# Large tiles at multiples of 256 bytes, and new tables of how far weight splits run ahead, in a two-layer encoder trunk

## The chip, the cores and the metric

The kernel runs on one core of a Trainium2 chip. The metric is the device time of one execution in microseconds (us). Before the change the median of three runs is 920.38 us (919.2 to 921.86). The engines are called PE (TensorE matmul), PEld (its weight loads), DVE (VectorE), ACT (ScalarE), POOL (GpSimd) and SP (SyncE, which only issues transfers here).

## What is computed

The reference takes 256 tokens of width 1024 through two layers. Each layer is a feed-forward network (FFN), an attention mix, and a second FFN, each behind an RMS norm and added to the residual; a final norm follows.

```
x = x + 0.5 * swiglu(rms_norm(x, ffn1_norm[l]), ffn1_w_gate[l], ffn1_w_up[l], ffn1_w_down[l])
proj = rms_norm(x, mix_norm[l]) @ w_in[l]            # 1024 -> 2304
out_a = windowed_gqa_sink(qa, ka, va, sink[l], slopes_a)
out_b = differential_attention(qb, kb, vb, lam, slopes_b)
x = x + concatenate([out_a, norm(out_b)]) @ w_out[l]  # 1024 -> 1024
x = x + 0.5 * swiglu(rms_norm(x, ffn2_norm[l]), ffn2_w_gate[l], ffn2_w_up[l], ffn2_w_down[l])

def swiglu(h, w_gate, w_up, w_down):                  # 1024 -> 2816 -> 1024
    return (jax.nn.silu(h @ w_gate) * (h @ w_up)) @ w_down
```

Everything is float32. The weights are about 41 million numbers, of which the four FFNs hold 35 million.

## The kernel before, in words

**Splits.** A float32 weight tile (`raw`, 128 partitions x 2048 numbers, 8 KB a partition, six buffers) is loaded from HBM and cut in two halves. Each half becomes two tiles of 4 KB a partition of the type float32r (`w`, from the pool `s4` of 28 buffers): ACT casts the raw half into the high part (`act.copy`, in the profile CAST w<-raw), and DVE subtracts that from the raw half for the low part (TENSOR_TENSOR w<-raw,w). One product of a chunk of 128 rows is then three matmuls: high by high, low by high, high by low (`tokens`, `prod`). This pair of instructions is called a split below.

**Groups of seven products.** An FFN has 2816 hidden columns, in groups of 512 (`ffn_specs`, `ffn`). For the groups in `SEVEN` gate and up are computed for the two halves of tokens with seven block products instead of eight (`seven`, `by_seven`, `by_sevens`). With a and d the two halves of the rows of gate, and b and c those of up, the weights wanted are a, d, a+b, a+b+c, b+c, c and a+b+c+d. The sums are made in place in the raw tiles: b is added into a by a transfer that POOL issues (`gather`, an adding DMA, raw<-in_ffn_w_up_dram from POOL), which waits until both halves of a are split; c into b by another; c into a+b (`plus(c, a)`) and d into a+b+c (`plus(d, a)`) by an addition on DVE (raw<-raw,raw). PE's order in such a group is a, dn1, d, dn0, ab, abc, bc, c, abcd (for layer 0's first FFN from its second group on, for the other three FFNs from the first, where dn1 begins with the second group): dn0 and dn1 are down-projections of hidden columns of groups before, 24 matmuls each, the others 12 each.

**Evacuations.** Between products ACT and DVE empty PSUM banks: ACT copies bank A to bank Q and starts silu from it (COPY ps<-ps, ACTIVATE tmp<-ps,r), DVE forms u0 and u1 (tmp<-ps,tmp and tmp<-xy,tmp) and the hidden activations (s<-tmp,hr,tmp); PE transposes these, and ACT and DVE split the result (`turn_one`: CAST s<-xy, then s<-xy,s on DVE, of which PE needs the low part in dn0).

**What sets the order.** Program order on ACT and DVE is fixed by the order in which Python writes it. Splits are numbered by halves, and `ahead(n)` writes all splits, additions, adding DMAs and loads up to half n that are not yet written. Between two evacuations `go()` calls `ahead` with the next number of a row of the table `LEAD`: rows `next`, `more` and `last` serve the first, middle and last group of seven products, with the number of the FFN (0 to 3) behind; rows `open` and `close` serve the first and last steps of an FFN, through `lead` and `weights`. A larger number puts more splits before the evacuation that follows. PE's own order does not depend on the tables.

```
def go(table=None):
    if table is not None:
        upto[0] = 2 * at["use"] - (2 if table == "next" else 0)
        more[0] = iter(LEAD[table + str(which)])
    ahead(upto[0] + next(more[0]))
```

**Places.** Tiles stand in a partition in the order of their pools: `const`, `wp` (raw), `s4` (weights, hidden activations, normed inputs), `tp` (tmp, q and v, where the sums of inputs lie, and small ones). The constants end so that the first raw tile begins at byte 32160 of a partition, 160 bytes past a multiple of 256; the raw and `s4` tiles and the `tmp`, `q` and `v` tiles all stand 160 past one.

Of the kernel before, what the change touches and what calls it, by code (L numbers as in the profile page):

```python
# [9 lines left out]
F32 = mybir.dt.float32  # L10
# [4 lines left out]
P = 128  # L15
# [16 lines left out]
ORDER = (("a", "d", "dn0", "ab", "abc", "bc", "c", "abcd"),  # L32
         ("a", "dn1", "d", "dn0", "ab", "abc", "bc", "c", "abcd"))
LEAD = dict(start=(2, 7, 8, 6),
            open0=(2, 0, 0, 2, 3, 6, 8, 6, 5, 6, 1, 10, 1, 5, 7, 6, 8, 0),
            next1=(10, 10, 14, 14, 14, 17, 19, 19, 20, 24),
            next2=(10, 10, 14, 14, 14, 17, 19, 19, 20, 24),
            next3=(10, 10, 14, 14, 14, 17, 19, 19, 20, 24),
            more0=(1, 9, 9, 11, 15, 15, 19, 19, 19, 23, 25),
            more1=(7, 8, 8, 9, 9, 14, 18, 18, 19, 19, 20),  # L40
            more2=(7, 8, 8, 9, 9, 14, 18, 18, 19, 19, 20),
            more3=(7, 8, 8, 9, 9, 14, 18, 18, 19, 19, 20),
            last0=(7, 8, 8, 15, 15, 15, 15, 17, 19, 19, 19),
            last1=(3, 7, 7, 9, 14, 14, 14, 17, 20, 20, 23),
            last2=(3, 7, 7, 9, 14, 14, 14, 17, 20, 20, 23),
            last3=(3, 7, 7, 9, 14, 14, 14, 17, 20, 20, 23),
            open1=(1, 6, 7, 3, 4, 11, 5, 9),
            open2=(10, 7, 6, 8, 2, 0, 9, 8),
            open3=(9, 3, -1, 1, 5, 1, 9, 9),
            close0=(10, 5, 11, 1, -1, 8, 11, 2, 8, 12, 0, -1, 3),  # L50
            close1=(1, 8, 12, 3, 3, 7, 7, 12, 6, 9, 10, 6, 1),
            close2=(1, 8, 12, 3, 3, 7, 7, 12, 6, 9, 10, 6, 1),
            close3=(1, 8, 12, 3, 3, 7, 7, 12, 6, 9, 10, 6, 1),
            mix=(10, 0, 0, 0, 11, 3, 2, 6, 8, 9, 5, 1, 3, 0, 3, 5, 2, 2, 4, 5, 4, 8, 1, 10, 4, 9))


# [1 line left out]
def trunk(ctx: ExitStack, tc: tile.TileContext, x, n1, g1, u1, d1, nm, w_in, sink,  # L58
# [23 lines left out]
    const = ctx.enter_context(tc.tile_pool(name="const", bufs=1))  # L82
    wp = ctx.enter_context(tc.tile_pool(name="wp", bufs=1))
    s4 = ctx.enter_context(tc.tile_pool(name="s4", bufs=N_S4))
    tp = ctx.enter_context(tc.tile_pool(name="tp", bufs=1))
    ps = ctx.enter_context(tc.tile_pool(name="ps", bufs=1, space=bass.MemoryType.PSUM))

    uid = [0]

# [493 lines left out]
    lsum = const.tile([P, 2, DEPTH], F32, name="lsum")  # L583
    nlam = const.tile([P, DEPTH], F32, name="nlam")
    gsub = const.tile([P, DEPTH], F32, name="gsub")
    slopeA = [2.0 ** -(h + 1) for h in range(8)]
    slopeB = [2.0 ** -(2 * (h + 1)) for h in range(4)]
    lam_init = [0.8 - 0.6 * math.exp(-0.3 * l) for l in range(DEPTH)]
# [748 lines left out]
```

## Time and profile before

The profiled execution took 919.88 us, of which the span from the first to the last instruction is 918.1.

| what | value |
|---|---|
| median of three runs | 920.38 us |
| profiled execution, and its span | 919.88 us, 918.1 us |
| ACT casts of weights (CAST w<-raw) | 457, 404.4 us busy |
| DVE low parts of weights (w<-raw,w) | 458, 477.7 us busy, 55.0 us idle before them |
| DVE additions of raw tiles | 30, 68.6 us busy |
| adding DMAs from POOL | 30 of 1024 KB, median 12.0 us from issue to landing |
| moved by DMA | 200.83 MB, mean 219 GB/s |

Busy shares say how long an engine worked, not what the end waits for. Matmuls overlap in time, so their pace is read from how many fit into a stretch. A transfer's time to landing includes its wait behind others on the same 16 DMA engines.

The four FFNs lie, in the span, from the start to about 172 us, from about 300 to 440, 480 to 610 and 755 to 911 us; the mixes lie between the first two and between the last two.

### The profile page before, as it was taken

The page shows a single profiled execution, that of the slowest core. Times are in us where ns is not written, and L with a number is a line of the kernel's source. Part 1 is how long each engine was busy: PE and PEld are TensorE (multiplying, and loading weights), DVE is VectorE, ACT ScalarE, POOL GpSimd, SP SyncE. Part 2 cuts the span into 40 slices and gives each one's busy share as a digit, 9 for nine tenths or more (in the row PEclk, how much of TensorE's full clock was granted, in tenths as well). Part 3 has the DMA queues.
Part 4 walks back from the last instruction along what each step waited for, and adds up shares of the span by engine and source line. Part 5 has one row for each costly group of instructions (what it writes and reads, how often), then busy time and mean ns, then how long its engine had stood idle before and what let it go on. Part 6 is the DMA issues. An engine that isn't in the chain of part 4 may idle for free.

```text
span 918.1 us, 12062 instructions
## 1 busy us (share of the span) xinstructions
PE 905.3 (99%) x4468; PEld 749.2 (82%) x4468; DVE 779.4 (85%) x1058; ACT 610.6 (67%) x970; POOL 61.4 (7%) x79
## 2 busy tenths in 40 slices
PE   9999999999999999999999999999999999999997
PEld 7888888888878888888888877888888888887786
DVE  5878989979896899989768898997888978989884
ACT  6847667666676667668456676676667776667660
POOL 0411010000001011010010010000000010010001
PEclk9999999999999999999999999999999999999999
DMA  9997898953156698899855898899501865898841
GB/s 328 344 257 225 267 241 286 314 133 140 47 197 172 172 259 256 252 251 346 296 106 182 217 291 259 224 357 262 176 36 48 305 143 176 210 297 265 213 156 47
DMA packets 114331, 200.83 MB, mean 219 GB/s; under 512 B 3678, under 2 KB 31648, under 8 KB 114272
## 3 DMA queue, kind: packets, MB, share of 16 engines
q1 hardware_dynamic: 97616, 167.66, 53.9%
q0 software_dynamic: 16096, 31.75, 19.5%
q8 instruction: 35, 0.57, 0.3%
q10 hardware_dynamic: 560, 0.66, 0.2%
q14 instruction: 24, 0.20, 0.1%
HBM read 199.00 MB, written 1.05 MB: 218 GB/s over the span
## 4 chain that ended last, share of the span: by engine, by line
PE 67%; DVE 13%; DMA 11%; issue 4%; ACT 4%; SPq 0%; POOLq 0%; POOL 0%; DVEq 0%; ACTq 0%
PE ps L73 48%; PE xy L73 19%; DMA raw<-in_ffn_w_up_dram 10%; DVE w L73 8%; DVE raw L73 3%; ACT w L73 3%; DVE s L73 1%; DMA xk<-in_x_dram 1%; DVE tmp L73 1%; ACT s L73 0%; SPq L187 0%; ACT junk L73 0%; ACT tmp L73 0%; DVE xk L73 0%; POOLq L1332 0%
## 5 line engine op out<-in xcount | busy, mean ns | idle before, releaser
L73 DVE TENSOR_TENSOR w<-raw,w 128x1024 fp32r<-128x1024 f32 (+1 forms) x458 | 477.7, 1097 | 55.0 <-ACT w L73 49.3
L73 PE MATMUL ps<-w,s 128*128 128x512 f32 (+1 forms) x1974 | 461.1, 390 | 1.5 <-ACT ps L73 1.4
L73 ACT CAST w<-raw 128x1024 fp32r<-128x1024 f32 (+1 forms) x457 | 404.4, 952 | 75.7 <-DVE raw L73 50.8
L73 PEld LDWEIGHTS ps<-w,s 128*128 128x128 f32 x1974 | 364.4, 188 | 81.0 <-ACT ps L73 3.1
L73 PE MATMUL xy<-w,s 128*128 128x512 f32 x600 | 143.4, 392 | 0.0
L73 PEld LDWEIGHTS xy<-w,s 128*128 128x128 f32 x600 | 111.5, 188 | 23.1
L73 PE MATMUL ps<-w,q 128*128 128x512 f32 x396 | 96.1, 392 | 2.4 <-DVE w L73 1.3
L73 PEld LDWEIGHTS ps<-w,q 128*128 128x128 f32 x396 | 73.8, 188 | 20.5 <-DVE w L73 4.1
L73 PE MATMUL ps<-s,w 128*128 128x512 f32 (+1 forms) x384 | 69.8, 338 | 0.0
L73 DVE TENSOR_TENSOR raw<-raw,raw 128x2048 f32<-128x2048 f32 x30 | 68.6, 2287 | 0.5
L73 PEld LDWEIGHTS ps<-s,w 128*128 128x128 f32 x384 | 58.7, 188 | 8.4
L73 POOL DMA_DIRECT2D raw<-in_ffn_w_up_dram x30 | 38.9, 1346 | 365.6 <-DVE w L73 292.0
L73 ACT ACTIVATE s<-ps,gcol 128x256 fp32r<-128x256 f32 (+1 forms) x80 | 31.4, 479 | 42.6 <-PE ps L73 42.6
L73 PE MATMUL xy<-w,v 128*128 128x512 f32 x180 | 43.2, 389 | 0.0
L73 ACT ACTIVATE tmp<-ps,r 128x512 f32<-128x512 f32 x34 | 22.9, 687 | 29.0 <-PE ps L73 28.6
L73 PEld LDWEIGHTS xy<-w,v 128*128 128x128 f32 x180 | 33.8, 188 | 7.0
L73 DVE SCALAR_TENSOR_TENSOR s<-ps,gcol,s 128x256 fp32r<-128x256 f32 x48 | 20.4, 478 | 20.2 <-ACT s L73 20.2
L73 ACT ACTIVATE s<-s,negm 128x256 f32<-128x256 f32 x64 | 31.8, 498 | 5.3 <-DVE negm L73 5.3
L73 PE MATMUL xy<-w,q 128*128 128x512 f32 x144 | 34.6, 389 | 0.0
L73 PEld LDWEIGHTS xy<-w,q 128*128 128x128 f32 x144 | 27.0, 188 | 5.6
L73 ACT CAST q<-tmp 128x512 fp32r<-128x512 f32 x20 | 12.4, 621 | 19.7 <-DVE tmp L73 19.4
L73 POOL TENSOR_TENSOR r<-ms,mhalf 128x2 f32<-128x2 f32 x6 | 5.1, 849 | 298.9 <-DVE ms L73 298.9
(131 smaller groups left out, 584.4 us busy)
## 6 DMA issues: line engine op xcount, KB each, us to landing
raw<-in_ffn_w_down_dram SPq DMA_DIRECT2D x44, 1024.0 KB, 7.2
raw<-in_ffn_w_gate_dram SPq DMA_DIRECT2D x39, 1024.0 KB, 5.6
raw<-in_ffn_w_up_dram SPq DMA_DIRECT2D x39, 1024.0 KB, 6.9
raw<-in_ffn_w_up_dram POOLq DMA_DIRECT2D x30, 1024.0 KB, 12.0
raw<-in_w_in_dram SPq DMA_DIRECT2D x14, 1024.0 KB, 8.5
raw<-in_ffn_w_gate_dram SPq DMA_DIRECT2D x8, 512.0 KB, 7.1
raw<-in_ffn_w_up_dram SPq DMA_DIRECT2D x8, 512.0 KB, 8.1
raw<-in_w_in_dram SPq DMA_DIRECT2D x8, 512.0 KB, 8.5
```

The lines of the kernel that those rows point to most:

```text
L73: ins = issue(*a, **k)
```

## The change

Two tiles that nothing reads or writes are added: 152 numbers (608 bytes) at the end of the constants, so that the first raw tile begins at byte 32768, and 64 numbers (256 bytes) at the head of `tp`. All `raw`, `s4`, `tmp`, `q` and `v` tiles then begin at multiples of 256 bytes. And the rows of `LEAD` are replaced, except `start` and `mix`; where FFNs 1 to 3 shared the numbers of a row, each has its own now.

```diff
-            open0=(2, 0, 0, 2, 3, 6, 8, 6, 5, 6, 1, 10, 1, 5, 7, 6, 8, 0),
+            open0=(7, 4, -1, 0, 6, 0, -1, 0, 5, 4, 10, 5, 5, 4, -1, 9, -1, -1),
...
-            more2=(7, 8, 8, 9, 9, 14, 18, 18, 19, 19, 20),
+            more2=(6, 8, 8, 10, 11, 15, 18, 19, 20, 20, 20),
...
+    tp.tile([P, 64], F32, tag="edge", bufs=1, name="edge_t")
...
+    const.tile([P, 152], F32, name="edge")
```

Three places show what the rows do. All are in layer 1's first FFN (FFN 2), between its second and third group of seven products, some 528 to 556 us into the span. Numbers in names count tiles as they are made, and differ between the two kernels for the same tile.

First, DVE in the third group. `raw_4656` before and `raw_4659` after are the tile that holds a, then a+b, then a+b+c; `s_968`, `s_969` before and `s_970`, `s_971` after are the transposed hidden activations. Before:

```order
L73 TENSOR_TENSOR w_4955<-raw_4656,w_4954 128x1024
L73 TENSOR_TENSOR s_968_4962<-xy_4434,s_968_4962 128x512
L73 TENSOR_TENSOR s_969_4969<-xy_4435,s_969_4969 128x512
L73 TENSOR_TENSOR w_4973<-raw_4656,w_4972 128x1024
L73 TENSOR_TENSOR raw_4656<-raw_4656,raw_4819 128x2048
L73 TENSOR_TENSOR w_5016<-raw_4656,w_5015 128x1024
```

And DVE at the same place after the change:

```order
L73 TENSOR_TENSOR w_4955<-raw_4659,w_4954 128x1024
L73 TENSOR_TENSOR w_4959<-raw_4659,w_4958 128x1024
L73 TENSOR_TENSOR raw_4659<-raw_4659,raw_4821 128x2048
L73 TENSOR_TENSOR s_970_4969<-xy_4436,s_970_4969 128x512
L73 TENSOR_TENSOR s_971_4976<-xy_4437,s_971_4976 128x512
L73 TENSOR_TENSOR w_4980<-raw_4659,w_4979 128x1024
```

The second split of a+b and the addition of c now stand before the two low halves of the hidden activations, which stood before them. The same swap stands in the second group of this FFN and in the second and third group of layer 0's second FFN.

Second, ACT at the end of the second group and the start of the third. `ps_4433` before and `ps_4435` after are bank Q. Before:

```order
L73 CAST w_4813<-raw_4656 128x1024
L73 COPY tmp_4835<-xy_4434 128x512
L73 COPY ps_4433<-ps_4432 128x512
L73 CAST w_4852<-raw_4656 128x1024
L73 ACTIVATE tmp_4885<-ps_4433,r_4335 128x512
L73 CAST w_4887<-raw_4663 128x1024
```

And ACT at the same place after the change:

```order
L73 CAST w_4817<-raw_4659 128x1024
L73 COPY tmp_4837<-xy_4436 128x512
L73 CAST w_4839<-raw_4659 128x1024
L73 COPY ps_4435<-ps_4434 128x512
L73 CAST w_4859<-raw_4713 128x1024
L73 ACTIVATE tmp_4891<-ps_4435,r_4333 128x512
```

The cast of the second half of a now stands before the copy into bank Q, and the cast of the next raw tile before the silu that reads Q once PE has added to it.

Third, DVE at that same end of the second group. `raw_4345` before and `raw_4343` after hold a+b+c and then a+b+c+d; the first row's raw tile is c. Before:

```order
L73 TENSOR_TENSOR w_4782<-raw_4563,w_4781 128x1024
L73 TENSOR_TENSOR raw_4345<-raw_4345,raw_4488 128x2048
L73 TENSOR_TENSOR w_4802<-raw_4563,w_4801 128x1024
L73 TENSOR_TENSOR w_4806<-raw_4345,w_4805 128x1024
L73 TENSOR_TENSOR w_4810<-raw_4345,w_4809 128x1024
```

And DVE there after the change:

```order
L73 TENSOR_TENSOR w_4784<-raw_4574,w_4783 128x1024
L73 TENSOR_TENSOR w_4788<-raw_4574,w_4787 128x1024
L73 TENSOR_TENSOR raw_4343<-raw_4343,raw_4490 128x2048
L73 TENSOR_TENSOR w_4810<-raw_4343,w_4809 128x1024
L73 TENSOR_TENSOR w_4814<-raw_4343,w_4813 128x1024
```

The second split of c has moved from behind the addition of d to before it.

More of the change, by code (lines that the diff above doesn't have):

```diff
@@ L34 @@
 LEAD = dict(start=(2, 7, 8, 6),
-            open0=(2, 0, 0, 2, 3, 6, 8, 6, 5, 6, 1, 10, 1, 5, 7, 6, 8, 0),
[L36 to L40, printed above, removed]
-            more2=(7, 8, 8, 9, 9, 14, 18, 18, 19, 19, 20),
-            more3=(7, 8, 8, 9, 9, 14, 18, 18, 19, 19, 20),
@@ L43 @@
[L43 to L51, printed above, removed]
@@ L52 @@
-            close2=(1, 8, 12, 3, 3, 7, 7, 12, 6, 9, 10, 6, 1),
-            close3=(1, 8, 12, 3, 3, 7, 7, 12, 6, 9, 10, 6, 1),
+            open0=(7, 4, -1, 0, 6, 0, -1, 0, 5, 4, 10, 5, 5, 4, -1, 9, -1, -1),
+            next1=(10, 10, 14, 14, 16, 19, 19, 19, 23, 23),
+            next2=(10, 10, 14, 14, 15, 19, 20, 20, 20, 20),
+            next3=(1, 9, 14, 14, 14, 16, 17, 19, 19, 25),
+            more0=(7, 9, 9, 13, 13, 15, 18, 19, 19, 22, 24),
+            more1=(2, 9, 9, 13, 13, 15, 19, 19, 20, 20, 22),
@@ new lines @@
+            more2=(6, 9, 9, 10, 11, 15, 18, 19, 20, 20, 20),
+            more3=(2, 7, 8, 9, 14, 15, 18, 19, 21, 21, 25),
+            last0=(4, 8, 8, 9, 12, 14, 16, 17, 20, 21, 24),
+            last1=(1, 8, 8, 14, 14, 14, 15, 18, 20, 21, 22),
+            last2=(6, 8, 8, 10, 12, 14, 16, 17, 17, 19, 23),
+            last3=(7, 7, 7, 9, 11, 14, 17, 17, 17, 19, 21),
+            open1=(4, 2, 8, 0, -1, 9, 9, 5),
+            open2=(9, 4, -1, 2, -1, 11, 8, 5),
+            open3=(3, 8, 8, 4, 6, 0, 9, 7),
@@ L54 @@
+            close0=(4, 10, 6, 12, 10, 11, 11, 7, 6, 11, 6, 2, 4),
+            close1=(9, 10, 12, 7, 5, 7, 7, 9, 6, 7, 8, 6, 3),
+            close2=(12, 6, 4, 7, 7, 3, 2, 10, 8, 10, 0, 3, 9),
+            close3=(12, 10, 11, 12, 11, 11, 10, 10, 12, 10, 9, 12, 12),
             mix=(10, 0, 0, 0, 11, 3, 2, 6, 8, 9, 5, 1, 3, 0, 3, 5, 2, 2, 4, 5, 4, 8, 1, 10, 4, 9))
```

## The prediction

> **What bounds the kernel now.** I read the page first, then the chain of work that ended last, then who waited for whom by engine, then single stretches of the timeline.
>
> ```profile
> span 918.1 us, 12062 instructions
> PE 905.3 (99%) x4468; PEld 749.2 (82%) x4468; DVE 779.4 (85%) x1058; ACT 610.6 (67%) x970; POOL 61.4 (7%) x79
> PE 67%; DVE 13%; DMA 11%; issue 4%; ACT 4%; SPq 0%; POOLq 0%; POOL 0%; DVEq 0%; ACTq 0%
> 778.36 10.88 PE ps L73 x48
> 907.03 4.24 PE L73 MATMUL ps<-w,s 128*128 128x256 f32 x34
> 887.89 0.87 PE ps L73 x8
> L73 PE MATMUL ps<-w,s 128*128 128x512 f32 x1938 | 456.8, 392 | 1.5 <-ACT ps L73 1.4
> ...
> L73 PE MATMUL xy<-s,w 128*128 128x512 f32 x32 | 11.5, 394 | 0.0
> ```
>
> The first three rows are the page's; then two pieces of the chain with a row of PE's timeline between them; then the first and the last of the seven groups of PE's instructions by shape that have 512 columns. TensorE's 99% says little, since ends of matmuls are modelled; its pace says more. 48 matmuls of 512 columns take 10.88 us, 226.7 ns each. The seven groups hold 3482 of them (789 us), and with the smaller ones (transposes at 0.87 / 8 = 109 ns, matmuls of 256 columns at about 120 ns, some attention work) PE needs about 891 us at its own pace. Its first matmul starts about 1 us into the span (the wait for `wake` below) and its last ends at 907.03 + 4.24 = 911.3. So some 19 us are not pace, and most of those are fixed: the start, changes between transposes and matmuls, small attention matmuls. What splits that come too late can cost is this:
>
> ```profile
> PE ps L73 <- ACT ps L73: 1.4, 2, 0.8
> PE ps L73 <- DVE w L73: 1.3, 3, 0.5
> PE ps L73 <- DVE wake L73: 1.0, 1, 1.0
> PE ps L73 <- ACT w L73: 0.9, 1, 0.9
> 531.74 2.88 PE L73 MATMUL xy<-w,v 128*128 128x512 f32 x12
> 535.19 2.11 PE L73 MATMUL ps<-w,s 128*128 128x512 f32 x8 [0.57 <-ACT ps L73]
> ```
>
> Four rows of PE's waits (us in total, times, longest), then two of its timeline. Without the start they are 3.6 us over six waits. A wait costs more than the idle time shown: from 531.74 to 535.19 are 3.45 us for twelve matmuls that need 2.72, so 0.73 are lost where 0.57 are shown. Six times 0.16 more, and some 2 us, my estimate, of waits too short for that view, make about **6.6 us that a table can win**. PE is the bound; VectorE stands close behind it in the stages of seven products, and nowhere else does PE wait for splits:
>
> ```profile
> 484.00:609.00 125.00, 123.11 (x551) 100.34 (x552) 112.33 (x104) 86.31 (x105) 7.70 (x6) 1.00 0.84 245
> DVE w L73 <- ACT w L73: 10.8, 13, 1.4
> 551.72 2.30 DVE raw L73
> 584.14 2.30 DVE raw L73
> ```
>
> This is the window of layer 1's first FFN (PE, PEld, DVE, ACT, POOL, clock, DMA share, GB/s), VectorE's wait there, and two pieces of the chain: the same addition in the third and in the fourth, last group of seven products. VectorE works 112.3 us and waits 10.8 of 125; DMA is busy 84%. A group has 132 matmuls and 8 transposes, 29.9 + 0.9 = 30.8 us of PE; the two additions lie 32.4 apart. Those 1.6 us a group are the loop split of `a`, adding DMA, split of `ab`, addition, split of `abc`, next group.
>
> **The change part by part.** No instruction is added or removed; order on SyncE, GpSimd and TensorE stays, DMA issues too. ScalarE and VectorE do the same work, with 142 of VectorE's 601 other instructions standing before or after another number of splits, mostly by one or two.
>
> *Splits drawn ahead (gain).* These rows are VectorE's and ScalarE's timelines and the chain near one group change:
>
> ```profile
> 538.17 0.75 DVE L73 SCALAR_TENSOR_TENSOR s<-tmp,hr,tmp 128x512 f32<-128x512 f32 x1
> 539.90 1.23 DVE L73 TENSOR_TENSOR w<-raw,w 128x1024 fp32r<-128x1024 f32 x1 [0.98 <-ACT w L73]
> 537.84 9.14 DMA raw<-in_ffn_w_up_dram
> 547.05 1.05 ACT L73 CAST w<-raw 128x1024 fp32r<-128x1024 f32 x1 [1.95 <-DMA raw<-in_ffn_w_up_dram]
> 555.13 2.36 DVE L73 TENSOR_TENSOR w<-raw,w 128x1024 fp32r<-128x1024 f32 x2 [1.12 <-ACT w L73]
> ```
>
> VectorE idles 0.98 us at 539.90 because the cast it needs stands behind an activation that waits for PE; now that cast goes first. It idles 1.12 at 555.13 because nothing stands between the addition and the split that needs a cast of its result; now two evacuations do. The second split of `a` goes ahead of one evacuation (0.6 us) and the adding DMA starts after it. Against it, the second addition of a group (for `abcd`) loses the split that stood behind it, and one cast's time (1.05) is idle there. The balance is about 1 us of idle less a group, against an excess of 1.6 here: at most the 6.6 us, if every wait goes.
>
> *Evacuations put back (cost).* What stood first must now wait:
>
> ```profile
> 549.27 1.28 DVE L73 TENSOR_TENSOR s<-xy,s 128x512 fp32r<-128x512 f32 x2
> 551.72 2.29 DVE L73 TENSOR_TENSOR raw<-raw,raw 128x2048 f32<-128x2048 f32 x1
> 547.12 3.45 PE L73 MATMUL ps<-w,s 128*128 128x512 f32 x14
> 534.56 0.58 ACT L73 COPY ps<-ps 128x512 f32<-128x512 f32 x1
> ```
>
> Queued behind the moved split (1.14 us from start to start) and the addition (2.29) are the low halves of the hidden activations (front part, first place); PE wants them twelve matmuls after 547.12, at 549.84, plus one, and the first of the two is there at about 549.95. With unchanged landings they come 3.4 us later, and everything PE has queued waits: 3.3 us here, 2 to 3 by the same reckoning at three more places of this kind (the second group of this FFN, the second and third of layer 0's second FFN). This is not a toll for every group: a PE that is 3 us late no longer waits for `abc`. Next, ScalarE's copy at 534.56, for which PE already waits 0.57, stands behind one more cast (0.95 us) and after an addition that now lets one split (1.14) go first (second and third place): 2.1 us more, of which the same lateness covers part. Reckoned on by hand through each FFN, about +2 in layer 0's second, +1 in layer 1's first, -0.5 in layer 1's second, where no addition moves, and some +2 for small shifts in openings and closings: **+2 to +6 us in all, or nothing** if the weights come 2 us earlier. That the order can be free shows in layer 0's first FFN, which has it already; VectorE and PE there:
>
> ```profile
> 65.72 2.29 DVE L73 TENSOR_TENSOR raw<-raw,raw 128x2048 f32<-128x2048 f32 x1
> 67.93 0.68 DVE L73 TENSOR_TENSOR s<-ps,s 128x512 fp32r<-128x512 f32 x1
> 69.50 5.60 PE L73 MATMUL ps<-w,s 128*128 128x512 f32 x24
> ```
>
> The low halves come behind the addition and are done by 69.2, 0.3 us before PE's 24 matmuls want them.
>
> *Alignment.* The first raw tile moves from byte 32160 of a partition (160 past a multiple of 256) to 32768, and the other large tiles with it.
>
> ```profile
> q1 hardware_dynamic: 97616, 167.66, 53.9%
> q0 software_dynamic: 16096, 31.75, 19.5%
> DMA to landing us min/median/max: 9.1/12.0/15.4
> ```
>
> Per packet, q1 takes 0.539 x 16 x 918.1 us / 97616 = 81 ns, q0 (the adding DMAs) 178. No large tile of this trace lies aligned, so the price is unknown. Bounds: no difference; or a median adding DMA (six of them in this FFN, 12.0 us) that lands like the quickest (9.1), 2.9 us earlier. A loss has no reason: the same bytes go to the same partitions. I take the middle, about 1.5 us earlier, which with the 0.6 us above is the 2 us that makes the moved evacuations free: then splits and addition are done before PE's transposes have come.
>
> [...]
>
> *Sum.* The profiled execution took 919.88 us, 0.5 below the median of 920.38. From the 6.6 us I take 5: the waits for `w` and for ScalarE's copies in all three FFNs go, the short ones stay, and evacuations cost little since weights lead. 919.9 - 5 = **915 us**. With nothing left of the waits 913, with half 917.
>
> **The rivals.**
>
> *Evacuations late (slower).* Landings stay where they are; the addition ahead of the low halves makes PE wait in the second and third groups. It decides as soon as adding DMAs land less than about 2 us earlier. For it: the cushion at 549.95 is 0.1 us, and nothing but the landing makes up for 3.4. Against it: each FFN pays once, and later waits vanish. 919.9 + 4.5 = 924.5, from 923 to 928.
>
> *No difference.* PE waits move from weights to evacuations, an early start for a late one; or the moves touch only instructions with cushions. 920, from 917.6 to 923.
>
> *Alignment sets PE's pace.* 34 matmuls of 256 columns in 4.24 us, less the last one's 0.28 of duration, are 120 ns each; 512 columns take 226.7, so every matmul carries 2 x 120 - 226.7 = 13.3 ns that do not depend on columns. If that came from the old starts, 3482 x 13.3 ns = 46 us would be PE's to win, until VectorE (112.3 of 125 us) stops it: about 890. Against it: nothing in the trace ties these 13.3 ns to addresses. [...]
>
> *The change does not do what it says.* As built, every raw, weight and working tile starts at a multiple of 256; that leaves only that it is without effect, which is the case above.
>
> **How the numbers follow.** Forecast 0.48, evacuations late 0.25, no difference 0.23, PE's pace 0.04. What a measurement can tell from no change is 0.3%, 2.8 us. Faster is the forecast and PE's pace, 0.52; same 0.23; slower 0.25. The forecast's own range is 911 to 917.6. From 905 to 925.5 leaves out PE's pace, a forecast with a bonus from transfers (0.03) and the slower case's tail (0.07): 0.14.
>
> **What would show it.** Right: adding DMAs with a median near 10.5 us and packets of q0 under 178 ns; VectorE's wait for casts near 8 us in that FFN; PE's waits for `w` and copies under 1.5 us in all; additions 31 us apart. Wrong: waits of PE for VectorE's `s` of 2 to 3 us early in the groups (evacuations late); packets of 81 and 178 ns as before with the same waits (no difference); 48 matmuls in less than 10.6 us (PE's pace). The forecast falls if landings do not move and PE waits for `s`.

## The result, and the profile after

The changed kernel takes **925.38 us** (median of four runs, 924.92 to 925.79) against 920.73 of before beside it (919.2 to 921.86): a ratio of 1.0062, with a 95% interval of 1.0039 to 1.0085. It is slower by 0.6%; the forecast was 915. Its profiled execution took 925.0 us, of which the span is 923.2, 5.1 more than before.

In the diff ahead of the prediction the new row `more2` is misprinted: it reads (6, 9, 9, 10, 11, 15, 18, 19, 20, 20, 20).

The page of the changed kernel: span, engines, the two large queues, the chain, and VectorE's low parts and PE's largest group.

```profile
span 923.2 us, 12057 instructions
...
PE 906.3 (98%) x4468; PEld 750.1 (81%) x4468; DVE 780.0 (84%) x1058; ACT 609.3 (66%) x970; POOL 63.2 (7%) x79
...
q1 hardware_dynamic: 97616, 167.66, 52.1%
q0 software_dynamic: 16096, 31.75, 19.7%
...
PE 72%; DVE 13%; DMA 6%; issue 5%; ACT 4%; SPq 0%; POOLq 0%; POOL 0%; DVEq 0%; ACTq 0%
...
L73 DVE TENSOR_TENSOR w<-raw,w 128x1024 fp32r<-128x1024 f32 (+1 forms) x458 | 476.8, 1098 | 49.1 <-ACT w L73 48.4
L73 PE MATMUL ps<-w,s 128*128 128x512 f32 (+1 forms) x1974 | 461.4, 390 | 5.4 <-DVE s L73 3.9
```

The work is the same: every engine is busy as long as before. VectorE idles 49.1 us ahead of its low parts instead of 55.0, so splits did come sooner. But PE's largest group now idles 5.4 us instead of 1.5, and what ends it is VectorE's `s`. PE's waits by what ended them (us in total, times, longest):

```profile
PE ps L73 <- DVE s L73: 3.9, 4, 1.4
PE ps L73 <- ACT ps L73: 1.5, 2, 0.9
PE ps L73 <- DVE w L73: 1.2, 3, 0.5
PE ps L73 <- ACT xy L73: 1.2, 2, 1.0
...
PE xy L73 <- DVE s L73: 0.6, 1, 0.6
PE ps L73 <- ACT w L73: 0.6, 1, 0.6
```

The three waits that were to go (copies 1.4, `w` from VectorE 1.3, from ScalarE 0.9) are still 1.5, 1.2 and 0.6. New are 4.5 us for `s` and 1.2 for ScalarE's copies into `xy`; 1.0 of these stands early in FFN 1, at 322.04 us, where two casts now stand ahead of the copy. PE's own order is the same in both kernels, so the start of the same matmul in the two traces can be subtracted; this "lateness" tells where the 5 us arise:

| matmul that starts before at | place | late by, us |
|---|---|---|
| 167.84 | end of FFN 0 | 0.2 |
| 371.70 | FFN 1, third group | 3.3 |
| 440.20 | end of FFN 1 | 2.0 |
| 550.17 | FFN 2, third group | 4.2 |
| 619.72 | end of FFN 2 | 1.8 |
| 841.04 | FFN 3, last groups | 5.9 |
| last | end | 5.5 |

FFN 1 costs about 1.9 us (it loses 1.2 at that copy and 1.5 at the third group, and wins some back), FFN 2 nothing on balance (it loses 2.4 at its third group and wins that back), FFN 3 about 3.5. The place of the moved low halves, layer 1's first FFN, on the timeline of the changed kernel:

```profile
549.02 2.36 DVE L73 TENSOR_TENSOR w<-raw,w 128x1024 fp32r<-128x1024 f32 x2 [0.34 <-ACT w L73]
549.22 1.03 PE L73 MATMUL xy<-ident,s 128*128 128x128 f32 x8
550.01 3.21 PE L73 MATMUL ps<-w,s 128*128 128x512 f32 x13
551.42 2.29 DVE L73 TENSOR_TENSOR raw<-raw,raw 128x2048 f32<-128x2048 f32 x1
553.63 1.28 DVE L73 TENSOR_TENSOR s<-xy,s 128x512 fp32r<-128x512 f32 x2
554.37 3.90 PE L73 MATMUL ps<-w,s 128*128 128x512 f32 x16 [1.16 <-DVE s L73]
```

The transposes end at 550.25; the low halves start at 553.63, behind two splits and the addition, and PE waits 1.16 us for the first. This is the rival called "evacuations late", in its own place.

### The profile page after: what moved, and what is told of

Read it like the earlier page. It is cut to its first block, busy times and chain, and to the rows that moved or that the text cites. A ratio compares the mean times of both kernels' runs of the same rounds, so it can differ in the third digit from the quotient of the medians.

```text
span 923.2 us, 12057 instructions
## 1 busy us (share of the span) xinstructions
PE 906.3 (98%) x4468; PEld 750.1 (81%) x4468; DVE 780.0 (84%) x1058; ACT 609.3 (66%) x970; POOL 63.2 (7%) x79
## 3 DMA queue, kind: packets, MB, share of 16 engines
q0 software_dynamic: 16096, 31.75, 19.7%
## 4 chain that ended last, share of the span: by engine, by line
PE 72%; DVE 13%; DMA 6%; issue 5%; ACT 4%; SPq 0%; POOLq 0%; POOL 0%; DVEq 0%; ACTq 0%
PE ps L73 51%; PE xy L73 21%; DVE w L73 8%; DMA raw<-in_ffn_w_up_dram 5%; DVE raw L73 4%; ACT w L73 3%; DVE s L73 1%; DMA xk<-in_x_dram 1%; ACT tmp L73 0%; DVE tmp L73 0%; ACT s L73 0%; SPq L188 0%; ACT xy L73 0%; DVE xk L73 0%; POOLq L1334 0%
## 5 line engine op out<-in xcount | busy, mean ns | idle before, releaser
L73 DVE TENSOR_TENSOR w<-raw,w 128x1024 fp32r<-128x1024 f32 (+1 forms) x458 | 476.8, 1098 | 49.1 <-ACT w L73 48.4
L73 ACT CAST s<-ps 128x512 fp32r<-128x512 f32 x21 | 11.8, 587 | 22.8 <-PE ps L73 22.8
## 6 DMA issues: line engine op xcount, KB each, us to landing
raw<-in_ffn_w_up_dram POOLq DMA_DIRECT2D x30, 1024.0 KB, 12.4
```

Source lines behind the costliest of these rows:

```text
L73: ins = issue(*a, **k)
```

## The experiments

All ratios are to the kernel before, run beside it on the same chip. The medians of before were 919.3 to 921.4 us. Single runs of one kernel spread by up to 13 us, so differences of 2 us between medians lie within overlapping intervals; there the trace of a single profiled run decides, and I say so.

### Which half of the change costs

The changed kernel with the old rows, and with the new rows but without the two tiles that shift places (`tables_alone`):

```diff
-    tp.tile([P, 64], F32, tag="edge", bufs=1, name="edge_t")
-    const.tile([P, 152], F32, name="edge")
```

> Only the places of the tiles change; all rows of the table are those of before. Order theory (the moved evacuations cost all): the time stays within 1.5 us of before, about 920; PE's waits are those of before (none for s). Alignment theory (the new places cost, by landings that come at other times): 923.5 to 926, most of what the whole change costs. Interaction theory (each alone costs nothing, both together cost): 920.

> The new rows of the table, with the tiles where they were before. Order theory: 924 to 926.5, with PE waiting for DVE's s in the second and third groups of FFNs 1, 2 and 3, 3 to 4 us in total as in the changed kernel; if alignment does bring loads nearer, a little more than the changed kernel, up to 927. Alignment theory: 919.5 to 921.5. Interaction theory: 920 to 921.5.

Places alone: 921.01 us, ratio 1.0001 (0.998 to 1.0021). Rows alone: 925.33, 1.0049 (1.003 to 1.0068). **The rows carry the loss; the places do nothing that the time shows.** The adding DMAs show why: in layer 1's first FFN their median landing is 12.0 before, 12.5 with the places alone, 12.1 with the rows alone, 11.2 with both. The places raise it when they change alone and lower it when the rows change with them, so no step goes with them. In layer 0's second FFN the four stand in the same order (11.0, 11.8, 11.3, 10.3), in the other two in another.

One thing was not as expected: in its profile, the kernel with the places alone waits 2.9 us for `s`, 2.0 of them in layer 0's first FFN, whose rows are those of before. An adding DMA lands late there; ScalarE and PE:

```profile
96.41 2.00 ACT L73 CAST w<-raw 128x1024 fp32r<-128x1024 f32 x2 [4.23 <-DMA raw<-in_ffn_w_up_dram]
...
102.83 7.08 PE L73 MATMUL ps<-w,s 128*128 128x512 f32 x23 [2.03 <-DVE s L73]
```

This FFN has the addition ahead of the low halves in both kernels, and the prediction showed it as an order that is free. It is free only when the adding DMA is quick. The one issued at about 84 us lands after 11.0, 11.2 and 11.7 us in three of the twenty profiles (`ffn13_back`, `load_alone`, `tiles_alone`), and there PE waits 1.1, 1.6 and 2.0 us for `s`; in the other seventeen it lands within 9.6 us, and PE does not wait there. Up to there `before` and `load_alone` are the same program, and it lands after 8.4 us in the one and 11.2 in the other; so this comes and goes between runs, and may add to their spread.

### Which FFN costs

The changed kernel with the rows of single FFNs as before (all rows whose number is that FFN's).

> The changed kernel with the rows of FFN 1 alone (layer 0's second) as before. Order theory: the 2.05 us that PE falls behind in that FFN go, 923.3 (922.5 to 924.2). Alignment theory: 925, no change. If lateness moves from one FFN into the next (an FFN that starts earlier waits more for the weights that are on the way), 924.5 to 925.5 too, with FFN 2 or 3 losing more than in the changed kernel.

> The changed kernel with the rows of FFN 3 alone (layer 1's second) as before. Order theory: the 3.6 us that PE falls behind in that FFN go, 921.7 (920.8 to 922.7). Alignment theory: 925, no change. If the 3.6 us come from weights that land later there (adding DMAs 13.7 against 12.4 us) whatever the order: 924.5 to 925.5.

> The changed kernel with the rows of FFNs 1 and 3 as before; those of FFNs 0 and 2 and the places stay as changed. If the costs of the FFNs add up, as PE's lateness in the trace says (FFN 0 and FFN 2 about nothing): 920 to 921.5, as before. If only the whole table or the places cost: 923 or more.

FFN 1 back: 924.14, 1.0034 (1.0015 to 1.0053). FFN 3 back: 922.26, 1.0018 (1.0 to 1.0036). Both back: 921.52, 1.0005 (0.9977 to 1.0033). The medians fall by 1.2, 3.1 and 3.9 from 925.4, where the lateness had said 1.9, 3.5 and 5.4. As far as medians with overlapping intervals can tell, the costs of the FFNs add up, and FFNs 0 and 2 cost nothing that can be measured.

### The swap alone, and the changed kernel without it

The swap is the first place of the change: second split of a+b and addition ahead of the low halves. Of a `more` row the second and third number decide it (8: behind, 9: ahead). `swap_alone` adds it to the kernel before, `no_swap` takes it out of the changed one:

```diff
 swap_alone (more1 and more2, from before)
-            more1=(7, 8, 8, 9, 9, 14, 18, 18, 19, 19, 20),
+            more1=(7, 9, 9, 9, 9, 14, 18, 18, 19, 19, 20),
 no_swap (more1 and more2, from the changed kernel)
-            more1=(2, 9, 9, 13, 13, 15, 19, 19, 20, 20, 22),
+            more1=(2, 8, 8, 13, 13, 15, 19, 19, 20, 20, 22),
```

> The kernel before, with that swap alone, in the middle groups of FFNs 1 and 2 (four places). If the swap costs what the changed kernel shows there: 1.5 to 3 us more than before, 922.3 to 924, PE waiting for s about 1 us at three or four places. By the full reckoning of the prediction (3.3 us at one place, 2 to 3 at the three others, each FFN paying once): 3 to 6 more, 924 to 927. If it is free: 920 to 921.5.

> The changed kernel, but in the middle groups of FFNs 1 and 2 the second split of a+b and the addition of c stand behind the low halves of the hidden activations again; nothing else is put back. If this swap is what costs in those FFNs: PE no longer waits for s at those four places (0.9 to 1.5 us each in the changed kernel), and as each FFN pays once, 1.5 to 3 us less than the changed kernel, 922.3 to 924. If the splits drawn ahead bring the gain that I forecast, and the swap alone took it back: 915 to 918. If the swap is free and the cost sits elsewhere: 925.

The swap alone: 925.46, 1.0044 (1.0021 to 1.0066), some 4 us, in the span of my reckoning by queue lengths (3 to 6). Yet without it the changed kernel is not faster but much slower: **931.67**, 1.0099 (1.0064 to 1.0134). All three theories missed that. The waits of `no_swap`, and its timeline at the end of FFN 2's third group:

```profile
PE ps L73 <- ACT ps L73: 8.6, 6, 2.3
```

```profile
568.45 2.28 DVE L73 TENSOR_TENSOR raw<-raw,raw 128x2048 f32<-128x2048 f32 x1
...
570.82 2.94 ACT L73 CAST w<-raw 128x1024 fp32r<-128x1024 f32 x3 [3.81 <-DVE raw L73]
...
573.67 0.57 ACT L73 COPY tmp<-xy 128x512 f32<-128x512 f32 x1
574.15 1.04 ACT L73 CAST w<-raw 128x1024 fp32r<-128x1024 f32 x1
...
575.10 0.58 ACT L73 COPY ps<-ps 128x512 f32<-128x512 f32 x1
...
575.73 1.65 PE L73 MATMUL ps<-w,s 128*128 128x512 f32 x3 [2.32 <-ACT ps L73]
```

The new rows put one more cast ahead of the copy into bank Q. In program order the copy, which needs only PE, stands behind casts that wait for the second addition (ScalarE idles 3.81 us for it, until 570.82); it starts at 575.10, and PE waits 2.32 us. The swap brings the additions forward and so hides this. The two moves belong together: in FFNs 1 and 2 the swap costs, the rest costs more without it, and each makes up for part of the other.

### Do landings decide what the swap costs?

The prediction set the cost of the swap to nothing if the adding DMAs land 2 us earlier. Here they move half:

```diff
-                pool.dma_start(raws[to], w[k], accum_op=ALU.add)
+                pool.dma_start(raws[to][:, 0:2], w[k][:, 0:2], accum_op=ALU.add)
```

> The kernel before, with adding DMAs that move half as much (one of the two 512-number halves of each b or c is not added: that part of the sums is left out). It is the base for the next two. Both theories: the adding DMAs land at least 3 us earlier (median under 9 us in place of 12), most waits for w go, 914 to 919.

> The changed kernel with adding DMAs that move half as much, as in the kernel before it. If the condition of the prediction holds (evacuations put back are free once the adding DMAs land some 2 us earlier): within 1.5 us of the kernel before with the same light DMAs, or faster by up to 3; no wait of PE for s of over 0.5 us. If the moved evacuations cost whatever the landings: 3 to 5 us slower than that kernel.

> The kernel before with the swap alone (second split of a+b and addition ahead of the low halves in the middle groups of FFNs 1 and 2) and adding DMAs that move half as much. If landings decide: within 1 us of the kernel before with light DMAs. If the swap costs by itself: about 4 us more, as it did with whole DMAs.

Light base: 912.34, 0.9902 (0.9864 to 0.994); its adding DMAs land in 7.8 us (median) in layer 1's first FFN instead of 12.0, and PE waits for nothing but its start. With the swap: **922.19**, 1.0008 (0.9989 to 1.0027); the changed kernel: 920.44, 0.999 (0.9973 to 1.0008). Landings 4 us earlier do not make the swap free; it costs 10 us by the medians (7.7 between the two profiled runs) where PE has no other wait that its lateness could absorb. VectorE and PE of `swap_light`, FFN 2:

```profile
544.88 8.03 DVE L73 TENSOR_TENSOR w<-raw,w 128x1024 fp32r<-128x1024 f32 x7
...
549.47 1.03 PE L73 MATMUL xy<-ident,s 128*128 128x128 f32 x8
...
552.94 2.29 DVE L73 TENSOR_TENSOR raw<-raw,raw 128x2048 f32<-128x2048 f32 x1
...
555.15 1.28 DVE L73 TENSOR_TENSOR s<-xy,s 128x512 fp32r<-128x512 f32 x2
...
555.89 4.41 PE L73 MATMUL ps<-w,s 128*128 128x512 f32 x18 [2.43 <-DVE s L73]
```

From 544.88 VectorE runs seven splits, the addition and the low halves without a gap. Nothing there waits for a transfer; the low halves wait for VectorE itself. PE's waits for `s` at the four places of the swap (second and third group of FFNs 1 and 2) say the same; the last row belongs to the next test:

| kernel | waits for `s` at the four places, us | sum |
|---|---|---|
| `swap_alone`, whole adding DMAs | 1.38, 2.42, 1.38, 2.40 | 7.6 |
| `swap_light`, landings 4 us earlier | 1.38, 2.42, 1.36, 2.43 | 7.6 |
| `swap_noadd`, without the addition | 0, 1.06, 0, 1.06 | 2.1 |

The landings change nothing at these four places.

### VectorE's queue

To see whether it is the queue, the piece of 2.29 us is taken out: the first addition of each group, c into a+b, in the kernel before and in the one with the swap alone.

```diff
-                     abc=Step(4, 512, None, prep=plus(c, a), src=a, free=[]),
+                     abc=Step(4, 512, None, src=a, free=[], added=True),
```

> The kernel before without VectorE's first addition of each group (c into a+b is left out, 15 times 2.29 us of VectorE). It is the base for the next. 908 to 917, since the loop over the adding DMA loses this piece.

> The kernel with the swap alone, without VectorE's first addition of each group (left out as in the kernel before it): the low halves of the hidden activations stand behind one more split (1.14 us) only. If what they wait for is VectorE's own queue: the swap costs 0 to 2 us against the kernel before it, in place of 4. If it is the cast on ScalarE or the landing: 4 us still.

Base 912.64, 0.9914 (0.9883 to 0.9945); with the swap 912.82, 0.9919 (0.9888 to 0.995). The swap that costs 4 us with the addition costs 0.2 without it; with four runs each the intervals leave room for some 4 us either way, so the medians speak for VectorE's queue without proving it. The traces say more: of 7.6 us of waits for `s` at the four places 2.1 are left (table above). Most of what PE waits for there is the addition in VectorE's queue. The moved split alone still costs something: `swap_noadd`'s one profile, its slowest run, falls 4.1 us behind its base's, which is that kernel's fastest.

### What FFN 3 loses

Here no addition moves. The first idea was evacuations again, and three kernels put back single numbers of its rows:

```diff
 ffn3_two
-            next3=(1, 9, 14, 14, 14, 16, 17, 19, 19, 25),
+            next3=(1, 9, 14, 14, 14, 17, 19, 19, 19, 25),
-            more3=(2, 7, 8, 9, 14, 15, 18, 19, 21, 21, 25),
+            more3=(2, 7, 8, 9, 14, 15, 18, 19, 21, 21, 21),
 ffn3_three (next3 as in the next two)
+            more3=(2, 8, 8, 9, 14, 15, 18, 18, 21, 21, 25),
 ffn3_ab
+            next3=(1, 9, 14, 14, 14, 16, 17, 19, 20, 25),
+            more3=(2, 7, 8, 9, 14, 15, 18, 18, 21, 21, 25),
 ffn3_load (next3 as in ffn3_ab)
+            more3=(2, 7, 8, 9, 14, 15, 18, 18, 19, 19, 20),
 load_alone (the kernel before)
-            more3=(7, 8, 8, 9, 9, 14, 18, 18, 19, 19, 20),
+            more3=(7, 8, 8, 9, 9, 14, 18, 18, 21, 21, 21),
```

> The changed kernel with two edits of FFN 3: in its first group the second split of the next a goes ahead of the evacuation u1 again (so the adding DMA is issued some 3 us earlier), and at the ends of its middle groups fewer splits are drawn ahead of the copy into bank Q (21 in place of 25). If these two are the cause: PE's lateness against before grows by less than 1.5 us in FFN 3 instead of 3.6, and the time is 922.5 to 924. If the cause is in its other rows (opening, closing, splits elsewhere): 924.5 to 925.5.

> The changed kernel with three places of FFN 3 put back: the copy into bank Q ahead of the cast of the second half of the next a (third and fourth group); no split of a+b between the two transposed halves of the hidden activations; one split more ahead of the silu of the second half in its first group. If these are the cause: PE's lateness against before grows by less than 1 us between 755 us and the end in place of 3.6, and the time is 921.5 to 923.5. If its opening, closing or the rest are the cause: 924.5 to 926.

> The changed kernel with two places of FFN 3 put back: the copy into bank Q ahead of the cast of the second half of the next a (third and fourth group), and one split more ahead of the silu of the second half in its first group; the split of a+b stays between the two transposed halves. If these two are the cause of FFN 3's loss: PE's lateness against before grows by 0.5 to 1.5 us between 755 us and the end in place of 3.6, and the time is 922 to 924. If not: 924.5 to 926.

925.71, 1.0046 (1.0024 to 1.0067); 926.62, 1.0054 (1.0031 to 1.0078); 926.63, 1.0058 (1.0029 to 1.0086). None wins anything. In the traces of the last two the waits that were aimed at are gone (lateness grows by about 0.3 and 0.9 us from 755 us to the third group, where in the changed kernel it grew by 2), but about 824 us PE waits 3.0 and 1.0 us for the split of a+b or for what stands behind it: the adding DMA is late. The rows of that transfer in the kernel before: the first adding DMA of the third group, the next load of gate, and how long the first took to land.

```profile
811.11 1.28 POOL L73 DMA_DIRECT2D raw<-in_ffn_w_up_dram  x1 [27.03 <-DVE w L73]
816.64 0.37 SPq L184 DMA_DIRECT2D raw<-in_ffn_w_gate_dram  x1
DMA to landing us min/median/max: 9.7/9.7/9.7
```

And in the changed kernel:

```profile
814.19 1.28 POOL L73 DMA_DIRECT2D raw<-in_ffn_w_up_dram  x1 [26.80 <-DVE w L73]
816.79 0.37 SPq L185 DMA_DIRECT2D raw<-in_ffn_w_gate_dram  x1
DMA to landing us min/median/max: 12.2/12.2/12.2
```

The load of gate waits for a raw buffer. The new rows draw the splits that free this buffer ahead of the evacuation u1 and the hidden activations (u0 stays in front), so the load starts 2.6 us behind the adding DMA instead of 5.5, and the adding DMA lands 2.5 us later. The profile's shares of the 16 DMA engines, from its issue to its landing: 58.8% for the queue of adding DMAs (q0) and 48.1% for that of the plain loads (q1), where before they were 74.3% and 35.8%. The seven profiles with whole adding DMAs and FFN 3's new rows up to here show 12.0 to 13.5 us, the five whole kernels with its old rows 9.6 to 10.4. Two runs test it:

> The changed kernel with FFN 3's row of middle groups put back at its end, so that the splits that free the raw buffer for the next load of gate stand where they stood before (behind the evacuations u0 and u1), with the copy into bank Q and the first group's one split as in the run before. If the early load of gate, 2.0 to 2.6 us behind the first adding DMA of a group, is what makes that DMA land late (12.0 to 13.5 us in place of 9.6 to 10.4 with 5.4 to 5.5 us between them): the gate load comes 4.5 us or more behind it, it lands within 10.5 us in the third group, PE's lateness against before grows by less than 1.5 us from 755 us to the end, and the time is 922 to 923.5. If not: 12 us again and 925 to 927.

> The kernel before with one row changed: in FFN 3's middle groups the two splits that free the raw buffer for the next load of gate stand ahead of the evacuations u0 and u1. If the early load is the cause: it is issued 2 to 3 us behind the first adding DMA of the third group, which lands in 12 to 13.5 us in place of 9.7, and the time is 1 to 3 us over before. If not: 9.7 us again, 920 to 921.5.

| kernel | load of gate behind the adding DMA, us | its landing, us | time, ratio to before |
|---|---|---|---|
| before | 5.5 | 9.7 | 1 |
| places alone | 5.5 | 9.7 | 1.0001 |
| changed | 2.6 | 12.2 | 1.0062 (1.0039 to 1.0085) |
| ffn3_ab | 2.0 | 12.2 | 1.0058 (1.0029 to 1.0086) |
| ffn3_load | 6.1 | 8.7 | 1.0036 (1.0015 to 1.0058) |
| load_alone | 2.0 | 11.2 | 1.0033 (1.001 to 1.0057) |

Without the early load (923.42 us) the adding DMA lands in 8.7 us, and on balance PE's lateness does not grow in FFN 3 (4.3 us at 661, 5.6 at 841, 4.0 at the end). The early load in the kernel before costs 4 us by the medians (923.65 against 919.3) and brings the landing to 11.2, a little under what I had expected; in the fourth group it is 13.2. `load_alone` also puts u1 and the hidden activations behind splits, but its new waits in the third and fourth group (0.73, 0.88 and 2.51 us) are for the casts of a+b that wait for the landing, or for what stands behind them. Against the changed kernel, `ffn3_load` is no more than 2 us faster and their intervals overlap; the trace, and the run in the other direction, carry this.

**A load that is released too early costs some 4 us by the medians when it is put alone into the kernel before. It is not the larger part of what FFN 3 loses in the changed kernel.** There PE and ScalarE show this:

```profile
792.74 0.66 PE L73 MATMUL xy<-ident,s 128*128 128x128 f32 x4 [0.62 <-DVE s L73]
813.10 3.26 PE L73 MATMUL ps<-w,s 128*128 128x512 f32 x13 [0.61 <-ACT ps L73]
829.44 2.81 PE L73 MATMUL ps<-w,s 128*128 128x512 f32 x11 [0.62 <-DVE s L73]
845.34 1.05 ACT L73 CAST w<-raw 128x1024 fp32r<-128x1024 f32 x1
846.28 0.59 ACT L73 COPY ps<-ps 128x512 f32<-128x512 f32 x1
846.92 3.26 PE L73 MATMUL ps<-w,s 128*128 128x512 f32 x13 [0.93 <-ACT ps L73]
```

The first wait is for hidden activations put behind two more splits; the second and the last are for the copy into bank Q, which stands behind one more cast. The first two come before the adding DMA is issued at 814.19. Only the third stands behind its late landing. Against `ffn3_back`, which has FFN 3's old rows, PE falls 4.9 us further behind: 2.8 at such evacuations (0.3 of them at a copy into `xy` at 774.97) and 1.9 at three waits behind late landings (829.44, 867.75, 869.01). And `after_light`, whose adding DMAs land in under 10 us throughout, falls 3.9 us behind `before_light` in FFN 3, 3.0 of them at the same four evacuations. So two causes lie one behind the other here: `ffn3_three` and `ffn3_ab` took these waits for evacuations away, and PE then waited for the landing instead; `ffn3_load` puts both back.

### A version that beats both

The light runs say that the loop over the adding DMA holds up to 9 us (921.35 to 912.34). Each adding DMA is cut in two, one for each half of the raw tile, in the kernel before; the whole sum is computed.

```diff
-                pool.dma_start(raws[to], w[k], accum_op=ALU.add)
+                for h in (0, 2):
+                    pool.dma_start(raws[to][:, h:h + 2], w[k][:, h:h + 2], accum_op=ALU.add)
```

> The kernel before, with each adding DMA cut in two of half the bytes, one for each half of the raw tile, so that the first half can start after the first half of a is split, and be split when it has landed. The whole sum is computed. If the loop over the adding DMA is what a group's 1.6 us over PE's pace come from, as the run with light DMAs says: first halves land some 4 us earlier, 912 to 917. If splits wait for both halves anyway, or the second issue costs: 920 to 922.

**914.55 us**, 0.9947 (0.9922 to 0.9972): faster than both. Issues and landings on its page:

```profile
raw<-in_ffn_w_up_dram POOLq DMA_DIRECT2D x60, 512.0 KB, 9.3
```

Sixty halves land in 9.3 us (median) where thirty whole ones took 12.0. That is 8.6 for the first halves and 11.1 for the second; the two together are there 12.2 us after the first issue, no sooner than a whole one, so what is won is the first half. About 812 us, the first half is issued 2.1 us ahead of the second, since it needs only the first half of a to be split. What PE still waits for most in this kernel are ScalarE's copies, 3.2 us in three waits.

## Why the prediction was wrong, step by step

- **What bounds the kernel**: right. PE's work, its pace and every engine's busy time are the same after; the 5 us are waits of PE (10.2 us in the view after, 5.5 in the one before).
- **Alignment** is the step that failed first. I took adding DMAs that land 1.5 us earlier, the middle between nothing and 2.9. Their median is 12.4 us after and 12.0 before, and per packet 0.197 x 16 x 923.2 us / 16096 = 181 ns after, 178 before: the lower bound was the truth. The places alone say the same (median 12.1). Only the plain loads gain (81 to 79 ns a packet on q1), and the time with the places alone (ratio 1.0001) shows that nothing waits for that.
- **Evacuations put back**: the cost was reckoned at 2 to 6 us and then set to nothing, on the ground that weights would lead; it came to about 5. That ground was wrong twice: the lead did not come, and the light runs show that it would not have helped, since in FFNs 1 and 2 the low halves stand behind VectorE's own work, not behind a transfer. I had the row that says so, 112.3 us busy of 125, and read it as a close second instead of as a queue with no room to catch up. The order of layer 0's first FFN, which I took for proof that it can be free, was free with landings of up to 9.6 us, and not with 11.0 and more.
- Its terms by FFN: +2 for FFN 1 was 1.9, of which 1.2 came from a copy into `xy` and not from the swap; +1 for FFN 2 was about 0. **-0.5 for FFN 3 was +3.5**: I took it that evacuations cost nothing where no addition moves, but casts and splits alone put off the copies into bank Q and the hidden activations there. I also asked only what each step moved past on each engine, not what a finished split sets free: which load its buffer releases. With some +2 for openings and closings the terms sum to 4.5, near the 5.4 that the lateness shows; as they are spread over the FFNs, that is luck.
- **Splits drawn ahead**: VectorE's idle time before low parts fell by 6 us, in layer 1's first FFN its wait for casts from 10.8 to 7.6 (the sign said near 8), but the waits of PE that were to vanish went from 3.6 to 3.3. VectorE's idle time was slack for its evacuations; at the places shown above, filling it with splits moved the wait to PE.
- **The rivals**: "evacuations late" at 924.5, 923 to 928, is what came, with more in it than it named: the addition ahead of the low halves accounts for the waits in FFNs 1 and 2, casts ahead of ScalarE's copies and an early load for the rest. Its condition (landings less than 2 us earlier) was met, but does not decide in FFNs 1 and 2, where the swap costs as much with landings 4 us earlier. "PE's pace" fell: 48 matmuls of 512 columns take 10.88 us after as before, with all tiles at multiples of 256.

What stays open: how much time the split costs without the addition (the runs without it are too few for a time; the waits say 2.1 of 7.6 us), what FFN 3 would lose if only the early load were put back in the changed kernel, and how much the small shifts in openings and closings carry.

## What to carry to other kernels

On an engine that is busy nine tenths of the time (VectorE here, 112.3 of 125 us), idle time ahead of one kind of work can be slack that another kind lives on (in `swap_alone` PE waited 7.6 us for the low halves at the four places): before moving work into it, list what stands behind it and who waits. When work is done earlier, ask what it sets free (a buffer, a semaphore), which transfer starts then, and what that transfer will share the DMA engines with (here a load 2.6 instead of 5.5 us behind an adding DMA, which landed in 12.2 us instead of 9.7). When putting one cause back wins nothing, look in the trace whether the wait is gone and another has taken its place. When a loop waits for one long transfer, try cutting the transfer so that its parts can start and be used as soon as their own halves are ready, before touching any order (here 914.55 us against 920.14 of before beside it).

## What the hardware showed beside this

A wait of PE can cost more than itself. In `swap_alone` PE waits 2.42 us for `s` at 376.62; the windows before, in and behind that wait (PE, PEld, DVE, ACT, POOL, clock, DMA share, GB/s):

```profile
369.00:374.20 5.20, 5.20 (x27) 4.04 (x26) 5.17 (x6) 3.09 (x5) 0.00 (x0) 1.00 1.09 252
374.20:376.60 2.40, 0.00 (x1) 0.00 (x0) 2.40 (x3) 1.10 (x2) 0.00 (x0) 0.99 1.05 402
376.60:380.00 3.40, 3.38 (x8) 2.71 (x9) 3.40 (x4) 3.40 (x5) 0.00 (x0) 0.50 0.47 174
380.00:384.00 4.00, 4.00 (x19) 3.29 (x19) 4.00 (x4) 0.84 (x1) 0.00 (x0) 1.00 0.27 56
```

The granted clock is 0.50 for 3.4 us; eight matmuls of 512 columns run in it, 425 ns each instead of 227, and 1.6 us more are lost. Such windows for five waits in the middle of the work:

| kernel | wait of PE, us | granted clock |
|---|---|---|
| `tiles_alone` | 2.03 | 0.97 in the 3.0 us that hold it, 0.55 for 3.6 us, then 1.00 |
| `swap_alone` | 2.42 | 0.99 in the 2.4 us before PE starts again, 0.50 for 3.4 us, then 1.00 |
| `swap_light` | 2.43 | 1.00 in the 10 us that hold it, and in the 8 us behind |
| `ffn3_three` | 3.0 | 0.88 in the 4.3 us that hold it, 0.53 for 6.1 us, then 1.00 |
| `ffn3_back` | 3.4 | 1.00 in the 4 us that hold most of it, 0.68 and 0.75 for 3 us each, then 1.00 |

In the kernel before (longest wait in the middle 0.9 us) and in the changed one (1.4) the clock is 1.00 in every window up to 905 us. So four of the five waits were followed by a lower clock, and the one of 2.43 us was not; whether this adds to the spread of the runs was not shown.

The packets of 512 bytes on q1 take 27 ns (median) in the trace of after where they take 32 in that of before; q1's packets of 1024, 2048 and 4096 bytes take 46, 84 and 159 in both, and those of 2048 bytes of the adding DMAs 178 in both. Which part of the change makes the shortest of these quicker, the two traces do not say.
